# Ragged softmax on one core: a 32-column clip beside a GpSimd fill, and whole-tile stores

## The chip, the core and the metric

The kernel runs on one NeuronCore of a Trainium2 chip. The core has five engines with an instruction queue each: TensorE (PE), VectorE (DVE), ScalarE (ACT), GpSimd (POOL) and SyncE (SP), and 16 DMA engines that carry all transfers between the chip's memory (HBM) and the on-chip memory (SBUF, 128 partitions). The metric is the device time of one execution in microseconds. Before the change it is 154.53 us, the median of three runs that lie between 154.44 and 154.55 us.

## What is computed

```python
x: (16, 8, 256, 256) float32        # batch, heads, rows, columns
lengths: (16,) int32                # each from 128 to 255, the same draw each time
result = zeros_like(x)
for b in range(batch):
    length = lengths[b]
    masked = x[b, :, :, :length]
    exp_masked = exp(masked - max(masked, axis=-1))
    result[b, :, :, :length] = exp_masked / sum(exp_masked, axis=-1)
```

Each row of 256 numbers becomes a softmax over its first `length` columns and zero behind them. The kernel leaves the maximum out: it takes exp of x itself, checks the sums at the end, and has a slow second pass for the case that a sum is out of bounds. With this input the second pass is not entered.

## The kernel before, in words

**Tiles.** One batch entry is one tile: 2048 rows, 16 on each of the 128 partitions, 256 columns, 2 MB, contiguous 16 KB on each partition. Sixteen tiles are worked through in positions 0 to 15 (`batch_of` says which batch entry stands at a position). They lie in eight slots of SBUF, position b in slot b modulo 8. `half` is 8 of the 16 rows of a partition, `quarter` is 4. The constant `ahead` is 4, `low` is 160, `mid` is 128, `late` is 13.

**Loads.** Position 0 is loaded by SP in two halves (line 145), positions 1 to 3 whole by POOL (line 196). From position 4 on, POOL loads only the first w columns of each row (line 168), w being the first of 160, 168, ..., 240 that is not under the length, or all 256. POOL reads the length into a register (line 210, which calls line 135), chooses w by branches, and waits until the load two positions earlier has landed (line 167) and until the tile that had the slot is stored (line 209). So two loads at most are under way, in one queue, q0. Columns from 160 on of slots 4 to 7 are set to zero once by four memsets (line 191), so that what stands behind w is finite.

**Compute.** For each tile DVE applies a mask (line 248): it takes the minimum of x and a line that is far above zero inside the length and far below it outside, over columns 128 to 255 of all 16 rows, 2048 elements for each partition. ACT takes exp (lines 374 and 377), for rows 4 to 15 one row at a time with the row's sum; DVE sums the first four rows itself (line 269). DVE then divides, half a tile at a time: a reciprocal of the sums (line 279) and a multiplication (line 282). The loop at line 292 fixes the order on DVE, for every position b but 1: divide(b, 0), mask(b + 1), divide(b, 1), total(b + 1). DVE works in this order alone, so divide(b, 1) stands behind the mask of the next tile, and with it behind the landing of the next load.

**Stores.** SP issues all stores (line 154) in order of position, into queue q1. `parts(b)` cuts a tile: position 0 in pieces of 2, 2, 4 and 8 rows, positions 1 to 7 in pieces of 8, 4 and 4, positions 8 to 12 and 15 in two halves, positions 13 and 14 whole. A piece waits until the half in which it ends is divided (line 149). Positions 2 to 12 also wait until the store two positions earlier has landed (line 153), and position 0 has a wait of its own: from its second piece on, until the mask of position 1 is through (line 151). At the end SP waits for the last stores (lines 158, 159, 407).

Of the kernel before, what the change touches and what calls it, by code (L numbers as in the profile page):

```python
# [9 lines left out]
F32 = mybir.dt.float32  # L10
BF16 = mybir.dt.bfloat16
I32 = mybir.dt.int32
ALU = mybir.AluOpType
AX = mybir.AxisListType.X
EXP = mybir.ActivationFunctionType.Exp
DVE = mybir.EngineType.DVE
# [5 lines left out]
def kernel(  # L22
# [6 lines left out]
    nc = tc.nc  # L29
    P = nc.NUM_PARTITIONS  # L30

    batch, heads, seq_q, seq_k = x.shape
    rows = heads * seq_q
    assert rows % P == 0
    nt = rows // P
    half = nt // 2
    quarter = nt // 4
# [8 lines left out]
    slots = 8  # L46
    ahead = 4
    assert ahead == 4 and slots == 8 and batch == 16

    def batch_of(pos):  # L50
        return pos + 1 if pos < ahead - 1 else {ahead - 1: 15, 15: 0}.get(pos, pos)
# [3 lines left out]
    low = widths[0]  # L55
    mid = seq_k // 2
    big = 1.0e30

    def parts(b):


        if b == 0:
            cuts = [0, 2, quarter, half, nt]
        elif b < 8:
            cuts = [0, half, half + quarter, nt]
        elif b < 13 or b == batch - 1:
            cuts = [0, half, nt]
        else:
            cuts = [0, nt]
        return [slice(i, j) for i, j in zip(cuts, cuts[1:])]  # L70

    pool = ctx.enter_context(tc.tile_pool(name="all", bufs=1))
    psum = ctx.enter_context(tc.tile_pool(name="psum", bufs=1, space=bass.MemoryType.PSUM))
    xt = pool.tile([P, slots, nt, seq_k], F32, name="xt")
    word64 = pool.tile([1, batch], mybir.dt.int64, name="word64")
    word = word64.bitcast(I32)
# [3 lines left out]
    len_s = pool.tile([P, batch], F32, name="len_s")  # L80
    iota_i = pool.tile([P, seq_k], I32, name="iota_i")
    down = pool.tile([P, seq_k], F32, name="down")
    row_sum = pool.tile([P, slots, nt], F32, name="row_sum")
    inv_sum = pool.tile([P, batch, nt], F32, name="inv_sum")
    warm = pool.tile([P, 1], F32, name="warm")
# [20 lines left out]
    with tc.tile_critical(no_gpsimd_drain=True):  # L106
# [9 lines left out]
        s_fill = sem("s_fill")  # L116
        s_v = sem("s_v")
        s_min = sem("s_min")
# [14 lines left out]
        def length(engine, at):  # L133

            return nc.values_load(
                at,
                engines=[engine],
                skip_runtime_bounds_check_because="compared with constants, never an address",
            )
# [3 lines left out]
        for h in range(2):  # L143
            s = slice(h * half, (h + 1) * half)
            nc.sync.dma_start(out=xt[:, 0, s], in_=x_f[batch_of(0), :, s]).then_inc(s_ld[h], 16)  # L145
        for b in range(batch):
            s_b = s_st[b % 2] if b < late else s_late if b < batch - 1 else s_last
            for s in parts(b):
                nc.sync.wait_ge(s_out, 2 * b + (s.stop - 1) // half + 1)
                if b == 0 and s.start == 2:  # L150
                    nc.sync.wait_ge(s_min, 3)
                if 2 <= b < late and s.start == 0:
                    nc.sync.wait_ge(s_b, 64 * (b // 2 + 2))
                nc.sync.dma_start(
                    out=out_f[batch_of(b), :, s, :], in_=xt[:, b % slots, s, :]
                ).then_inc(s_b, 16 * (1 if b == 0 else (s.stop - s.start) // quarter))
        for par in range(2):
            nc.sync.wait_ge(s_st[par], n_st[par])
        nc.sync.wait_ge(s_late, 64 * (batch - 1 - late))
# [3 lines left out]
        def pick(v, b, slot, par, ws, landed):  # L163

            if len(ws) == 1:
                w = ws[0]
                nc.gpsimd.wait_ge(s_sw[par], landed)
                nc.gpsimd.dma_start(  # L168
                    out=xt[:, slot, :, :w], in_=x_n[:, b, :, :w]
                ).then_inc(s_sw[par], 16)  # L170
                return
            m = (len(ws) - 1) // 2
            with nc.gpsimd.If(v <= ws[m]):
                pick(v, b, slot, par, ws[: m + 1], landed)
            with nc.gpsimd.Else():
                pick(v, b, slot, par, ws[m + 1 :], landed)
# [8 lines left out]
        nc.gpsimd.memset(ones_c, 1.0).then_inc(s_ones, 1)  # L185
        for par in range(2):
            nc.gpsimd.memset(seed[:, par : par + 1], 0.0).then_inc(s_st[par], 128)  # L187
        nc.gpsimd.wait_ge(s_v, 2)

        def fill(b):  # L190
            nc.gpsimd.memset(xt[:, b, :, low:], 0.0).then_inc(s_fill, 1)  # L191


        fill(ahead)
        for b in range(1, ahead):
            nc.gpsimd.dma_start(out=xt[:, b], in_=x_f[batch_of(b)]).then_inc(  # L196
                s_sw[b - 1] if b < 3 else s_ld[2], 16
            )
        nc.gpsimd.wait_ge(s_word, 16)
        for b in range(ahead + 1, slots):  # L200
            fill(b)
        nc.gpsimd.wait_ge(s_fill, slots - ahead)


        with nc.Fori(16, 16 * (batch // 2 - 1), 16, engines=[POOL]) as landed:
            for par in range(2):
                n = landed // 8 + (ahead - 2 + par)
                b = n % 15 if par == 1 else n
                nc.gpsimd.wait_ge(s_st[par], 4 * landed)
                v_len = length(POOL, word[0:1, bass.ds(2 * b, 1)])  # L210
                pick(v_len, bass.ds(b, 1), bass.ds(n % slots, 1), par, widths + [seq_k], landed)
# [11 lines left out]
        def step(ins):  # L223
            nonlocal v
            v += 1
            ins.then_inc(s_v, 1)
# [5 lines left out]
                out=down, in0=iota_i, scalar1=0.5, scalar2=-big, op0=ALU.add, op1=ALU.mult  # L232
            )
        )
        nc.vector.wait_ge(s_word, 16)
        nc.vector.tensor_copy(out=len_b, in_=word[:, ::2]).then_inc(s_lenb, 1)  # L236
        nc.vector.wait_ge(s_lenf, 1)
        step(
            nc.vector.tensor_scalar(  # L239
                out=len_s, in0=len_f, scalar1=big, scalar2=None, op0=ALU.mult  # L240
# [1 line left out]
        )  # L242
        nc.vector.wait_ge(s_v, v)

        def clip(b, s, lo, hi):

            t = xt[:, b % slots, s, lo:hi]
            return nc.vector.scalar_tensor_tensor(  # L248
                out=t,
                in0=down[:, None, lo:hi].to_broadcast([P, s.stop - s.start, hi - lo]),  # L250
                scalar=len_s[:, batch_of(b) : batch_of(b) + 1],
                in1=t,
                op0=ALU.add,
                op1=ALU.min,
            )

        def mask(b, s):
            if b == 0:
                nc.vector.wait_ge(s_ld[s.start // half], 16)
            elif b == ahead - 1:  # L260
                nc.vector.wait_ge(s_ld[2], 16)
            else:
                par = (b - 1 if b < ahead else b) % 2
                nc.vector.wait_ge(s_sw[par], 16 * max(b // 2, 1))
            clip(b, s, mid, seq_k).then_inc(s_min, 1)

        def total(b):
            nc.vector.wait_ge(s_lump, b + 1)
# [7 lines left out]
        def divide(b, h):  # L276
# [10 lines left out]
            ).then_inc(s_out, 1)  # L287

        mask(0, slice(0, half))
        mask(0, slice(half, nt))  # L290
        total(0)
        for b in range(batch):


            first = b != 1
            if first:
                divide(b, 0)
            if b + 1 < batch:
                mask(b + 1, slice(0, nt))
            if not first:  # L300
                divide(b, 0)
            divide(b, 1)
            if b + 1 < batch:
                total(b + 1)
# [14 lines left out]
        for k, (_, _, edge, op) in enumerate(checks):  # L319
            nc.vector.tensor_scalar(  # L320
                out=bad[:, k : k + 1],
                in0=ends[:, k : k + 1],
                scalar1=edge,
                scalar2=None,
                op0=op,
# [9 lines left out]
        with nc.vector.Else():  # L335
            with nc.Fori(0, batch, 1, engines=[DVE]) as i:
                nc.vector.wait_ge(g_ld, 16 * i + 16)
                nc.vector.scalar_tensor_tensor(
                    out=g_t,
                    in0=down[:, None, :].to_broadcast([P, nt, seq_k]),  # L340
                    scalar=len_s[:, bass.ds(i, 1)],
                    in1=g_t,
                    op0=ALU.add,
                    op1=ALU.min,
# [3 lines left out]
                    out=neg_max, in_=g_t, op=ALU.max, axis=AX, negate=True  # L348
# [5 lines left out]
                    out=g_t,  # L354
                    in0=g_t,
# [9 lines left out]
        with nc.Fori(0, batch // slots, 1, engines=[ACT]) as turn:  # L365
            for slot in range(slots):
                for h in range(2):
# [7 lines left out]
                    for j in range(h * half + lump * (1 - h), (h + 1) * half):  # L375
                        e = xt[:, slot, j, :]
                        ins = nc.scalar.activation(  # L377
                            out=e, in_=e, func=EXP, accum_out=row_sum[:, slot, j : j + 1]
# [5 lines left out]
        with nc.scalar.If(a_redo >= 1):  # L384
# [4 lines left out]
            with nc.Fori(0, batch, 1, engines=[ACT]) as i:  # L389
                nc.scalar.dma_start(out=g_t, in_=x_g[:, bass.ds(i, 1)]).then_inc(g_ld, 16)  # L390
                nc.scalar.wait_ge(g_v, 3 * i + 2)
                with nc.Fori(0, nt, 1, engines=[ACT]) as t:
                    e = g_t[:, bass.ds(t, 1), :]
                    nc.scalar.activation(
                        out=e,
                        in_=e,
# [41 lines left out]
```

## Time and profile before

| what | value |
|---|---|
| median of three runs | 154.53 us (154.44 to 154.55) |
| the profiled execution: span, first to last instruction | 152.8 us |
| outside the span, by the median | 1.7 us |
| DVE busy | 134.6 us, 107 instructions |
| ACT busy | 95.1 us |
| POOL busy | 21.3 us |
| moved by DMA | 61.57 MB (read 27.98, written 33.55), 403 GB/s over the span |

The span is one execution under the profiler; what it lacks to the measured time lies before its first and after its last instruction. The page of the profile gives the busy time of each engine, then the span in 40 slices with a digit for each (9 is 90% busy or more), then the DMA queues with packets, megabytes and the share of the 16 engines' time that their packets took. The lines themselves are shown below, where they are used.

### The profile page before, as it was taken

The numbers are of one execution on the slowest core, as the hardware profiler recorded it, in microseconds if no ns is written. First come the engines' busy times: TensorE is split into PE (matmuls) and PEld (weight loads), VectorE is DVE, ScalarE is ACT, GpSimd is POOL, SyncE is SP. The second block draws the span as 40 slices with busy tenths as digits, with TensorE's granted clock in tenths as the row PEclk, the third lists the DMA queues.
The fourth block names the chain that finished last, engine by engine and source line by source line (L and its number), as shares of the span: only waits on it lengthen the run. The fifth ranks groups of instructions, "written<-read, shape, count | busy, mean of one in ns | idle before, by whom it ended". The sixth has DMA issues, their size and how long they took to land.

```text
span 152.8 us, 818 instructions
## 1 busy us (share of the span) xinstructions
PE 0.3 (0%) x2; PEld 0.2 (0%) x2; DVE 134.6 (88%) x107; ACT 95.1 (62%) x402; POOL 21.3 (14%) x29
## 2 busy tenths in 40 slices
PE   0000000000000000000000000000000000000000
PEld 0000000000000000000000000000000000000000
DVE  1369999999999999999999999999999999999500
ACT  3096699339394967859393939577593939395000
POOL 4962110030303020030300220302000000000000
DMA  4999999999999999999999999999999999999994
GB/s 107 420 446 433 401 435 347 421 445 420 394 397 422 405 421 411 411 409 405 419 411 418 408 399 419 408 410 423 417 421 419 413 420 422 435 435 442 429 410 187
DMA packets 10646, 61.57 MB, mean 403 GB/s; under 512 B 898, under 2 KB 1010, under 8 KB 7058
## 3 DMA queue, kind: packets, MB, share of 16 engines
q1 hardware_dynamic: 5904, 35.65, 56.7%
q0 software_dynamic: 4736, 25.89, 41.9%
q14 instruction: 4, 0.03, 0.1%
q10 hardware_dynamic: 2, 0.00, 0.0%
HBM read 27.98 MB, written 33.55 MB: 403 GB/s over the span
## 4 chain that ended last, share of the span: by engine, by line
DVE 87%; DMA 5%; issue 1%; SPq 0%; PE 0%
DVE xt L282 48%; DVE xt L248 23%; DVE row_sum L269 12%; DMA xt<-in_x_dram 5%; DVE inv_sum L279 3%; DVE ends L317 0%; SPq L145 0%; DVE bad L320 0%; PE count L218 0%; DVE redo L328 0%; SPq L433 0%; SPq L106 0%
## 5 line engine op out<-in xcount | busy, mean ns | idle before, releaser
L377 ACT ACTIVATE xt<-xt 128x256 f32<-128x256 f32 x192 | 76.6, 400 | 0.2 <-DVE xt L248 0.2
L282 DVE TENSOR_TENSOR xt<-xt,inv_sum 128x2048 f32<-128x2048 f32 x32 | 73.3, 2292 | 1.1
L374 ACT ACTIVATE xt<-xt 128x1024 f32<-128x1024 f32 x16 | 16.9, 1056 | 42.8 <-DVE xt L248 42.8
L248 DVE SCALAR_TENSOR_TENSOR xt<-down,len_s,xt 128x2048 f32<-128x2048 f32 (+1 forms) x17 | 37.7, 2219 | 5.0 <-DMA xt<-in_x_dram 5.0
L377 ACT ACTIVATION_READ_ACCUMULATOR xt<-xt 128x1 f32 x192 | 35.9, 187 | 0.0
L168 POOL DMA_DIRECT2D xt<-in_x_dram x12 | 13.2, 1104 | 84.0 <-DMA xt<-in_x_dram 62.3
L269 DVE TENSOR_REDUCE row_sum<-xt 128x4 f32<-128x1024 f32 x16 | 19.4, 1210 | 0.0
L279 DVE RECIPROCAL inv_sum<-row_sum 128x8 f32<-128x8 f32 x32 | 6.3, 198 | 0.5
L191 POOL MEMSET xt<- 128x1536 f32 x4 | 5.4, 1398 | 1.1 <-DVE len_s L239 1.1
L361 ACT ACT_TABLE_LOAD x1 | 1.3, 1283 | 1.6 <-SPq L106 1.6
L196 POOL DMA_DIRECT2D xt<-in_x_dram x3 | 1.8, 590 | 0.0
L231 DVE TENSOR_SCALAR down<-iota_i 128x256 f32<-128x256 int32 x1 | 0.3, 300 | 1.6 <-POOL iota_i L181 1.6
L317 DVE TENSOR_REDUCE ends<-inv_sum 128x1 f32<-128x256 f32 x2 | 0.7, 408 | 0.0
L236 DVE CAST len_b<-word 1x16 bf16<-1x16 int32 x1 | 0.2, 164 | 0.4 <-DMA word<-in_lengths_dram 0.4
L239 DVE TENSOR_SCALAR len_s<-len_f 128x16 f32<-128x16 f32 x1 | 0.2, 176 | 0.3 <-PE len_f L216 0.3
L218 PE MATMUL count<-bad,ones_c 128*1 128x3 bf16 x1 | 0.2, 165 | 140.8 <-DVE bad L320 140.8
L181 POOL IOTA iota_i<- 128x256 int32 x1 | 0.3, 331 | 0.6 <-SPq L106 0.6
L328 DVE TENSOR_REDUCE redo<-count 1x1 f32<-1x3 f32 x1 | 0.1, 150 | 0.3 <-PE count L218 0.3
L320 DVE TENSOR_SCALAR bad<-ends 128x1 bf16<-128x1 f32 x3 | 0.3, 150 | 0.0
L187 POOL MEMSET seed<- 1x1 f32 x2 | 0.2, 225 | 0.0
L218 PEld LDWEIGHTS count<-bad,ones_c 128*1 128x1 bf16 x1 | 0.1, 79 | 140.8 <-DVE bad L320 140.8
L361 ACT ACTIVATE warm<-const-float32-0.0 128x1 f32<-128x1 f32 x1 | 0.2, 204 | 0.0
(10 smaller groups left out, 1.1 us busy)
## 6 DMA issues: line engine op xcount, KB each, us to landing
out_dram<-xt SPq DMA_DIRECT2D x20, 1024.0 KB
xt<-in_x_dram POOLq DMA_DIRECT2D x4, 2048.0 KB, 16.3
out_dram<-xt SPq DMA_DIRECT2D x15, 512.0 KB
xt<-in_x_dram POOLq DMA_DIRECT2D x3, 1728.0 KB, 16.7
out_dram<-xt SPq DMA_DIRECT2D x2, 2048.0 KB
xt<-in_x_dram POOLq DMA_DIRECT2D x2, 1600.0 KB, 16.0
xt<-in_x_dram POOLq DMA_DIRECT2D x2, 1280.0 KB, 14.7
xt<-in_x_dram SPq DMA_DIRECT2D x2, 1024.0 KB, 6.4
```

What stands on the lines that cost most here:

```text
L168: nc.gpsimd.dma_start(out=xt[:, slot, :, :w], in_=x_n[:, b, :, :w]).then_inc(s_sw[par], 16)
L191: nc.gpsimd.memset(xt[:, b, :, low:], 0.0).then_inc(s_fill, 1)
L196: nc.gpsimd.dma_start(out=xt[:, b], in_=x_f[batch_of(b)]).then_inc(s_sw[b - 1] if b < 3 else s_ld[2], 16)
L218: nc.tensor.matmul(count, lhsT=ones_c, rhs=bad, start=True, stop=True).then_inc(s_count, 1)
L248: return nc.vector.scalar_tensor_tensor(out=t, in0=down[:, None, lo:hi].to_broadcast([P, s.stop - s.start, hi - lo]), scalar=len_s[:, batc ...
L269: nc.vector.tensor_reduce(out=row_sum[:, b % slots, :lump], in_=xt[:, b % slots, :lump, :], op=ALU.add, axis=AX,).then_inc(s_exp[0], 1)
L279: step(nc.vector.reciprocal(out=inv_sum[:, b, s], in_=row_sum[:, b % slots, s]))
L282: nc.vector.tensor_tensor(out=t, in0=t, in1=inv_sum[:, b, s, None].to_broadcast([P, half, seq_k]), op=ALU.mult,).then_inc(s_out, 1)
L317: step(nc.vector.tensor_reduce(out=ends[:, k : k + 1], in_=values, op=op, axis=AX))
L361: nc.scalar.activation(out=warm, in_=nc.const_aps.tensor(0.0, (P, 1), F32), func=EXP)
L374: nc.scalar.activation(out=e, in_=e, func=EXP).then_inc(s_lump, 1)
L377: ins = nc.scalar.activation(out=e, in_=e, func=EXP, accum_out=row_sum[:, slot, j : j + 1])
```

## The change

The change has three parts.

- **The narrow mask.** For positions from 4 on DVE clips only 32 columns (`edge` = 160 - 128), which begin at the tile's length, or at 224 if that is less. DVE reads the first column into a register from a small tile `first_col`, which one new instruction computes at the start. What stands behind w is filled by GpSimd: right behind each narrow load POOL copies a constant of -1e30 over columns w to 255 of the 16 rows (for a full load, a dummy copy of one column). The mask waits for that fill on the semaphore `s_fill`. Of the four memsets at the start, one stays for slot 4, now with -1e30, and a small one makes the constant.
- **Whole stores.** `parts` cuts only positions 0 and 15, in two halves; all others are stored whole, with 16 KB on each partition.
- **No hold.** The wait of position 0's second piece for the mask of position 1 goes.

```diff
     def parts(b):
-        if b == 0:
-            cuts = [0, 2, quarter, half, nt]
-        elif b < 8:
-            cuts = [0, half, half + quarter, nt]
-        elif b < 13 or b == batch - 1:
+        if b in (0, batch - 1):
             cuts = [0, half, nt]
         else:
             cuts = [0, nt]
...
                 nc.sync.wait_ge(s_out, 2 * b + (s.stop - 1) // half + 1)
-                if b == 0 and s.start == 2:
-                    nc.sync.wait_ge(s_min, 3)
                 if 2 <= b < late and s.start == 0:
                     nc.sync.wait_ge(s_b, 64 * (b // 2 + 2))
...
                 nc.gpsimd.dma_start(
                     out=xt[:, slot, :, :w], in_=x_n[:, b, :, :w]
                 ).then_inc(s_sw[par], 16)
+                m = max(seq_k - w, 1)
+                nc.gpsimd.tensor_copy(
+                    out=xt[:, slot, :, w:] if w < seq_k else spent[:, : nt, None],
+                    in_=never[:, None, :m].to_broadcast([P, nt, m]),
+                ).then_inc(s_fill, 1)
                 return
...
-        nc.gpsimd.wait_ge(s_v, 2)
-        def fill(b):
-            nc.gpsimd.memset(xt[:, b, :, low:], 0.0).then_inc(s_fill, 1)
-        fill(ahead)
+        nc.gpsimd.wait_ge(s_v, 3)
+        nc.gpsimd.memset(xt[:, ahead, :, low:], -big).then_inc(s_fill, 1)
+        nc.gpsimd.memset(never, -big).then_inc(s_fill, 1)
...
-        for b in range(ahead + 1, slots):
-            fill(b)
-        nc.gpsimd.wait_ge(s_fill, slots - ahead)
+        nc.gpsimd.wait_ge(s_fill, 2)
...
+        step(
+            nc.vector.tensor_scalar(
+                out=first_col, in0=word[:, ::2],
+                scalar1=seq_k - edge, scalar2=0, op0=ALU.min, op1=ALU.max,
+            )
+        )
...
         def mask(b, s):
+            cols, n = slice(mid, seq_k), seq_k - mid
+            if b >= ahead:
+                k = batch_of(b)
+                cols, n = bass.ds(length(DVE, first_col[0:1, k : k + 1]), edge), edge
+                nc.vector.wait_ge(s_fill, b - ahead + 3)
...
-            clip(b, s, mid, seq_k).then_inc(s_min, 1)
+            clip(b, s, cols, n).then_inc(s_min, 1)
```

More of the change, by code (lines that the diff above doesn't have):

```diff
@@ L57 @@
     big = 1.0e30
+    edge = low - mid
     def parts(b):
-        if b == 0:
-            cuts = [0, 2, quarter, half, nt]
-        elif b < 8:
-            cuts = [0, half, half + quarter, nt]
-        elif b < 13 or b == batch - 1:
+        if b in (0, batch - 1):
             cuts = [0, half, nt]
@@ L82 @@
     down = pool.tile([P, seq_k], F32, name="down")
+    never = pool.tile([P, seq_k - low], F32, name="never")
+    spent = pool.tile([P, nt], F32, name="spent")
+    first_col = pool.tile([1, batch], I32, name="first_col")
     row_sum = pool.tile([P, slots, nt], F32, name="row_sum")
@@ L155 @@
                     out=out_f[batch_of(b), :, s, :], in_=xt[:, b % slots, s, :]
-                ).then_inc(s_b, 16 * (1 if b == 0 else (s.stop - s.start) // quarter))
+                ).then_inc(s_b, 16 * (s.stop - s.start) // quarter)
         for par in range(2):
@@ L236 @@
         nc.vector.tensor_copy(out=len_b, in_=word[:, ::2]).then_inc(s_lenb, 1)
+        step(
+            nc.vector.tensor_scalar(
+                out=first_col,
+                in0=word[:, ::2],
+                scalar1=seq_k - edge,
+                scalar2=0,
+                op0=ALU.min,
+                op1=ALU.max,
+            )
+        )
         nc.vector.wait_ge(s_lenf, 1)
@@ L243, with clip @@
         nc.vector.wait_ge(s_v, v)
-        def clip(b, s, lo, hi):
-            t = xt[:, b % slots, s, lo:hi]
+        def clip(b, s, cols, n):
+            t = xt[:, b % slots, s, cols]
             return nc.vector.scalar_tensor_tensor(
                 out=t,
-                in0=down[:, None, lo:hi].to_broadcast([P, s.stop - s.start, hi - lo]),
+                in0=down[:, cols][:, None, :].to_broadcast([P, s.stop - s.start, n]),
                 scalar=len_s[:, batch_of(b) : batch_of(b) + 1],
```

## The prediction, made before the changed kernel was run

> **What bounds the kernel now.** I read the page first: its head, its slices, its queues and its chain.
>
> ```profile
> span 152.8 us, 818 instructions
> ...
> DMA  4999999999999999999999999999999999999994
> ...
> q1 hardware_dynamic: 5904, 35.65, 56.7%
> q0 software_dynamic: 4736, 25.89, 41.9%
> ...
> DVE 87%; DMA 5%; issue 1%; SPq 0%; PE 0%
> ```
>
> The chain names DVE. But the DMA row is full in every slice but the ends, and the two queues take 98.6% of the 16 engines' span. So I cut the span into stages (columns: engine busy times, clock, DMA share, GB/s) and looked at the first and last packet.
>
> ```profile
> 15.00:127.00 112.00, 0.00 (x0) 0.00 (x0) 110.66 (x81) 77.45 (x329) 12.76 (x12) 1.00 1.02 412
> 127.00:144.00 17.00, 0.17 (x1) 0.08 (x1) 16.39 (x19) 10.21 (x47) 0.00 (x0) 1.00 1.02 432
> ...
> 1.14 0.86 SPq L145 DMA_DIRECT2D xt<-in_x_dram  x2
> ...
> q1 hardware_dynamic: 7, 0.06, 254.2%
> ...
> DMA packets 0, 0.00 MB, mean 0 GB/s; under 512 B 0, under 2 KB 0, under 8 KB 0
> ```
>
> The last two rows are the queue in 2.15 to 2.30 us (its first seven packets, 1.0 us after SP's issue at 1.14) and the queues in 151.3 to 152.8 (nothing). From 2.15 to 151.3 the engines carry packets without a gap, at a share of 1.02 (packets overlap a little). So the end is set by **DMA: 149.1 us of transfers**, with 2.15 us in front and 1.5 us behind. DVE is also nearly always busy, but its last store is only queued behind others: the stores waited for earlier stores 11 times, 86.6 us in all.
>
> ```profile
> SPq L153 <- DMA out_dram<-xt: 86.6, 11, 9.9
> ...
> DVE xt L248 <- DMA xt<-in_x_dram: 5.0, 2, 3.5
> ```
>
> The second row says that masks waited for loads only twice, at the start. So before, DVE never starves, and behind it stands a backlog of stores, which keeps DMA full to the end.
>
> **Part one, the narrow mask.** Rows of the groups by form (mean ns), then one tile on DVE in the chain.
>
> ```profile
> L248 DVE SCALAR_TENSOR_TENSOR xt<-down,len_s,xt 128x2048 f32<-128x2048 f32 x15 | 35.2, 2344 | 0.0
> L248 DVE SCALAR_TENSOR_TENSOR xt<-down,len_s,xt 128x1024 f32<-128x1024 f32 x2 | 2.6, 1284 | 5.0 <-DMA xt<-in_x_dram 5.0
> ...
> 131.61 2.26 DVE xt L248
> 133.87 0.12 DVE inv_sum L279
> ...
> 134.02 2.29 DVE xt L282
> 136.31 1.14 DVE row_sum L269
> ...
> 137.47 0.21 DVE inv_sum L279
> ...
> 137.71 2.29 DVE xt L282
> 140.00 0.12 DVE inv_sum L279
> ```
>
> The two sizes give 1.035 ns an element and 0.22 us fixed, so 512 elements take 0.75 us; 1.59 us goes, 12 times, 19.1 us of DVE. A tile costs DVE 8.39 us now (131.61 to 140.00) and 6.8 after. A tile costs DMA 2.10 MB of store and of load, without q0's four full ones, (25.89 - 4 x 2.10) / 11 = 1.6 MB: 3.7 MB at 412 GB/s is 9.0 us. DVE is therefore not what ends last, and by itself this gain is **worth nothing**. It does have an effect: DVE eats its backlog. How far loads lead the masks shows in two tiles:
>
> ```profile
> 19.49 0.54 POOL L168 DMA_DIRECT2D xt<-in_x_dram  x1 [3.81 <-DMA xt<-in_x_dram]
> ...
> xt<-in_x_dram POOLq DMA_DIRECT2D x1, 2048.0 KB, 20.1
> 47.61 2.34 DVE L248 SCALAR_TENSOR_TENSOR xt<-down,len_s,xt 128x2048 f32<-128x2048 f32 x1
> ...
> 106.21 1.15 POOL L168 DMA_DIRECT2D xt<-in_x_dram  x1 [6.97 <-issue]
> ...
> xt<-in_x_dram POOLq DMA_DIRECT2D x1, 1536.0 KB, 21.0
> ```
>
> Position 5 lands at 19.49 + 20.1 = 39.6 and is masked at 47.6: a lead of 8.0 us. Position 15 lands at 127.2 and is masked at 131.6: 4.4. Saving 1.59 a tile uses up 8 us after five tiles. From about position 9 each mask waits for its load.
>
> The new register load on DVE: the only one in this trace took 0.84 us (row below). It stands ahead of the waits, so it runs on DVE's sequencer beside the 2.29 us of the division in front, or during the wait for the load. Uncovered it costs 12 x 0.84 = 10.1 us of DVE, still less than 19.1, and 0.8 on the path at the very end. I take 0. The new wait for the fill holds divide(b, 1) behind it. The fill is issued right behind its load, which takes 13.4 us at least to land. Three memsets of 1536 elements took 4.04 us, 1.35 each; a copy of 16 to 1536 elements I put between 0.1 and 2.7 (twice that), covered either way. POOL has the room: it stands idle 84.0 us before its loads. The three memsets that go and the small instruction for `first_col` have SP's first loads beside them (q1 holds the engines alone until 7.6, a row below): 0.
>
> ```profile
> L135 DVEq TENSOR_LOAD <-redo x1: 842/842/842, 143.9 to 143.9; - x1
> ...
> DMA to landing us min/median/max: 13.4/16.8/21.0
> ...
> 6.12 4.04 POOL L191 MEMSET xt<- 128x1536 f32 x3
> ...
> L168 POOL DMA_DIRECT2D xt<-in_x_dram x12 | 13.2, 1104 | 84.0 <-DMA xt<-in_x_dram 62.3 <-issue 15.5 <-DMA out_dram<-xt 6.1
> ```
>
> **Part two, whole stores.** First the packets' price. Queue rows of three stretches: 49.5 to 55 (stores in 4 KB packets beside loads), 146.6 to 148.6 (8 KB, stores alone), 142 to 145.5 (16 KB, alone).
>
> ```profile
> q0 software_dynamic: 292, 1.18, 53.2%
> q1 hardware_dynamic: 289, 1.08, 48.6%
> ...
> q1 hardware_dynamic: 114, 0.85, 100.9%
> ...
> q1 hardware_dynamic: 94, 1.47, 97.8%
> ```
>
> Bytes over size give 264, 104 and 90 data packets; share x stretch x 16 over these gives 0.162, 0.310 and 0.609 us. A partition's 16 KB cost 0.310 + 2 x 0.162 = 0.634 us in positions 1 to 7, 0.620 in 8 to 12, and 0.609 whole. Each engine has 8 partitions: 7 x 8 x 0.025 + 5 x 8 x 0.011 = 1.84 us. Position 0 loses its two 2 KB packets (0.09 each by the same line): 8 x (2 x 0.09 + 0.162 - 0.310) = 0.2. In all **2.0 us less transfer**; bounds 1.5 and 2.5 from rounding of the rows.
>
> The Trainium skill, "SBUF — State Buffer", section "The DMA setup-cost knee", puts about 2 us on each transfer and asks for the largest single ones; 23 stores fewer would then bring an estimated 46 us by that page. The stretch 146.6 to 148.6 speaks against it: two stores meet there and the share stays at 100.9%, so a queued store pays nothing of the kind.
>
> Then who gets DMA. In 49.5 to 55 the two queues move 292 and 289 packets. In 47.5 to 49.5, with 8 KB stores, they move these:
>
> ```profile
> q1 hardware_dynamic: 65, 0.53, 63.6%
> q0 software_dynamic: 71, 0.31, 38.0%
> ```
>
> **The queues alternate packet by packet, whatever their size.** Against a narrow load's 4.4 KB (0.31 MB / 71) a 16 KB store packet takes 79% of the bytes, an 8 KB one 63%. While a whole store runs, a load crawls at about 90 GB/s. Nothing is lost by that while both queues hold work, but loads are late and stores early: the opposite of a backlog of stores.
>
> **What is late next.** With loads late, DVE stands at mask(b + 1), and behind it divide(b, 1), and behind that the whole store of b. (Before, the first half could go alone.) At the last load this costs DMA time: when position 15 lands, positions 14 and 15 are not stored, all else is or nearly is. Work until then is all but two stores (2 x 8 x 0.609 = 9.8): 2.15 + 149.1 - 2.0 - 9.8 = 139.5, and the landing is seen a little later (at the end of the run between 0 and 1.5 us, the stretch from the last packet to the end of the span); I take 0.3, so 139.8. Then mask 0.75, divide(14, 1) 2.44 by the chain above, 1.0 from issue to first packet: store 14 starts at 144.05. DMA idles **4.5 us**. Store 14 runs to 148.95. Divide(15, 0) ends at 143.0 + 1.14 + 2.55 = 146.7 and divide(15, 1) at 149.15; their halves start at 148.95 and 151.4 without a gap and end at 153.85. With 1.5 behind, the span is 155.35.
>
> **Part three, no hold** lets 1 MB of store run beside loads 2 and 3, 2.5 us at most (8 x 0.310); it makes DVE wait under 1 us early, where it has 19 us to spare: 0.
>
> **The sum:** -2.0 + 4.5 = +2.5 us on the profile's 152.8, and the same on the median, whose 1.7 us outside the span do not change: **157.0 us**.
>
> **Rivals.**
> *Backlog stays (faster).* If at the last landing 4.5 us of store packets are still queued, nothing idles and only the 2.0 us count: 152.5. That is so if loads keep their share, for instance if a 16 KB packet is cut at 4 KB before queues alternate. Against it speak the equal counts at 8 KB, and the stretch 17 to 23 us, where 16 KB loads ran beside small pieces of store:
>
> ```profile
> q0 software_dynamic: 155, 2.28, 93.2%
> q1 hardware_dynamic: 114, 0.23, 9.9%
> ```
>
> The bytes stood 10 to 1; with cuts at 4 KB, 2 KB pieces would have had a third. What speaks for it: no 16 KB store runs beside a narrow load in this trace, so the share there is extrapolated. The Trainium skill, "DMA: Bandwidth & Descriptors", section "SWDGE vs HWDGE vs iDMA", has a packet at 4096 B preferably, as "the DMA engine's context-switching boundary"; by that sentence the time would be this rival's, and the two rows do not bear it out. Chance 0.17.
> *Part of the gap (same).* Load 15 has only some 22 packets an engine (1.57 MB / 4.4 KB / 16). If it lands right behind load 14, store 13 is itself held (it starts 0.75 + 2.44 + 1.0 = 4.2 behind mask 14) and covers part. Mask 15 then follows divide(14, 0), 0.75 + 2.44 + 1.14 + 2.55 = 6.9 behind mask 14; store 14 starts at 6.9 + 4.2 = 11.1, store 13 ended at 4.2 + 4.9 = 9.1: 2.0 us idle there. With 2.0 saved: 154.5. Chance 0.11.
> *More gaps (slower still).* POOL asks for load n + 2 only when load n has landed, and q0's first packet came over 3.2 us behind its issue at 4.37 (below; 7.0 to 7.6 holds q1 alone). A narrow load alone takes about 3.9 us (1.6 MB at 412). If the request takes 4 to 5 us, each time that no store runs beside, q0 falls dry for up to 1 us, some four times: 159 to 161. Chance 0.10.
>
> ```profile
> 4.37 1.76 POOL L196 DMA_DIRECT2D xt<-in_x_dram  x3
> ...
> q1 hardware_dynamic: 31, 0.25, 99.8%
> ```
>
> **Chances and range.** My forecast with 1.5 to 2.5 saved and 3.5 to 5.5 idle, 155.5 to 158.5, has 0.62. Slower by over 0.2% (0.3 us, about what a measurement can tell) 0.72, within 0.11, faster 0.17. The range that leaves out no more than 2 in 10 takes in the part gap and stops ahead of the pure gain: 153.8 to 159.4.
>
> **What would show it.** Right: mask 0.75 us; masks from about position 9 on wait for loads; the last load lands at 135 or later instead of 127; a slice near 140 with DMA far under 9; equal packet counts with stores at 80% of the bytes. Wrong: DMA full to the end, or DVE's masks never waiting.

## The result, and the profile after

The changed kernel takes **159.02 us** (median of five runs, 158.89 to 163.42) against 154.53 us before: a ratio of 1.0286, with a 95% interval of 1.0272 to 1.0301. It is slower by 4.5 us where +2.5 us was forecast. The changed kernel has a second, slower state, 161 us and more, in some of its runs; the ratios leave it out, and the rows below are of the same kernel in a run of 159.38 us with a span of 157.8 us. These are the page's head, DMA slices and queues.

```profile
span 157.8 us, 915 instructions
...
DMA  4999999999999999999999999999999999995994
...
q1 hardware_dynamic: 2880, 35.65, 54.0%
q0 software_dynamic: 4736, 25.89, 43.1%
```

The same megabytes went through the same queues. Share times span gives the time that one engine spent on each queue: the stores' q1 took 86.6 us before (56.7% of 152.8) and 85.2 now, **1.4 less**; the loads' q0 took 64.0 and now 68.0, **4.0 more**. And one slice near the end is down to 5. The waits on DVE and the last piece of DMA in the chain:

```profile
DVE xt L255 <- DMA xt<-in_x_dram: 16.3, 9, 4.3
```

```profile
122.56 17.89 DMA xt<-in_x_dram
140.45 0.03 issue
140.48 0.02 DVEq L276
...
141.52 0.75 DVE xt L255
...
142.42 2.29 DVE xt L294
```

By this row masks wait for loads nine times, where before it was twice. The last load lands at 140.45 in place of 127.2. The narrow mask takes 0.75 us, but starts 1.07 us after the landing: DVE's sequencer works out the address of the 32 columns (rows of line 255 with a q) behind the wait. The stretch from 143 to 146 us, in the changed kernel and before (second last column the DMA share):

```profile
143.00:146.00 3.00, 0.00 (x0) 0.00 (x0) 2.96 (x3) 3.00 (x15) 0.00 (x0) 1.00 0.43 183
```

```profile
143.00:146.00 3.00, 0.17 (x1) 0.08 (x1) 0.60 (x6) 0.00 (x0) 0.00 (x0) 1.00 0.99 423
```

That is an idle stretch of 3.0 x (1 - 0.43) = 1.7 us, while DVE divides the second half of tile 14 (the row at 142.42) and ACT works on tile 15. So of the 5.0 us between the two spans, 2.6 are dearer transfers (4.0 - 1.4) and 1.7 the gap; about 0.7 is left over, in the overlap of packets and in smaller idle stretches behind the last landing.

### The profile page after: what moved, and what is told of

The parts are those of the page before. It is cut to its first block, busy times and chain, and to the rows that moved or that the text cites. A ratio compares the mean times of both kernels' runs of the same rounds, so it can differ in the third digit from the quotient of the medians.

```text
span 159.7 us, 915 instructions
## 1 busy us (share of the span) xinstructions
PE 0.3 (0%) x2; PEld 0.2 (0%) x2; DVE 126.4 (79%) x108; ACT 95.0 (59%) x402; POOL 33.5 (21%) x39
## 4 chain that ended last, share of the span: by engine, by line
DMA 84%; DVE 7%; issue 3%; POOL 1%; POOLq 1%; DVEq 0%; PE 0%; ACTq 0%; SPq 0%
DMA xt<-in_x_dram 83%; DVE xt L294 4%; POOL xt L193 1%; DMA word<-in_lengths_dram 1%; DVE row_sum L281 1%; POOLq L166 1%; DVE xt L255 0%; DVE ends L329 0%; DVE inv_sum L291 0%; DVEq L255 0%; POOLq L135 0%; DVE bad L332 0%; DVE len_s L246 0%; PE count L215 0%; PE len_f L213 0%
## 5 line engine op out<-in xcount | busy, mean ns | idle before, releaser
L294 DVE TENSOR_TENSOR xt<-xt,inv_sum 128x2048 f32<-128x2048 f32 x32 | 79.9, 2498 | 1.1
L255 DVE SCALAR_TENSOR_TENSOR xt<-down,len_s,xt (+2 forms) x17 | 22.2, 1305 | 23.5 <-DMA xt<-in_x_dram 19.0
L170 POOL COPY xt<-never 128x640 f32 (+6 forms) x11 | 15.1, 1373 | 0.0
L193 POOL MEMSET xt<- 128x1536 f32 x1 | 1.4, 1388 | 1.1 <-DVE len_s L246 1.1
L170 POOL COPY spent<-never 128x16 f32<-128x16 f32 x1 | 1.1, 1092 | 0.0
```

What stands on the lines that cost most here:

```text
L170: nc.gpsimd.tensor_copy(out=xt[:, slot, :, w:] if w < seq_k else spent[:, : nt, None], in_=never[:, None, :m].to_broadcast([P, nt, m]),).t ...
L193: nc.gpsimd.memset(xt[:, ahead, :, low:], -big).then_inc(s_fill, 1)
L255: return nc.vector.scalar_tensor_tensor(out=t, in0=down[:, cols][:, None, :].to_broadcast([P, s.stop - s.start, n]), scalar=len_s[:, batch ...
L294: nc.vector.tensor_tensor(out=t, in0=t, in1=inv_sum[:, b, s, None].to_broadcast([P, half, seq_k]), op=ALU.mult,).then_inc(s_out, 1)
```

## The experiments

Two theories went into the first four runs. **Theory A** is the prediction's: large store packets delay the loads, and DMA idles at the last load. **Theory B**: the cost lies in the new steps of the narrow mask. Ratios are to runs of the kernel before on the same chip, with the 95% interval.

**The changed kernel again**, unchanged.

> The changed kernel once more, for a profile of an ordinary run. Theory A (stores in 16 KB packets take four fifths of the DMA time while they run, loads come late, the mask of the next tile holds the division and the whole store, and DMA idles at the last load): 158.9 to 159.2 us, last load landed at 138 or later, masks waiting for loads, one idle stretch of DMA near the end of some 2 to 5 us. Theory B (the cost lies in the new steps of the narrow mask on DVE and GpSimd): the same time, and the sum of the waits of DVE that are not for a landing explains some 4 us.

It took 158.74 and 159.38 us. The gap is 1.7 us, a little under what A names. As B would have it, the profile has 4.5 us of waits of masks that it does not put down to a landing:

```profile
DVE xt L255 <- issue: 4.5, 2, 3.0
```

But both stand behind landings. The shorter is the last mask's, shown above. The longer ends with the mask of position 6 at 59.63 us, 0.35 us behind POOL's issue of the load that waits for the landing of the same tile. So after the start masks wait for their loads at positions 6 to 9 and 13 to 15, and these waits do not speak for B. The next runs test it by itself.

**The narrow mask alone.** The lines of `parts`, the hold and the semaphore increments are as before, all else as changed.

```diff
-        if b in (0, batch - 1):
-            cuts = [0, half, nt]
+        if b == 0:
+            cuts = [0, 2, quarter, half, nt]
+        elif b < 8:
+            cuts = [0, half, half + quarter, nt]
+        elif b < 13 or b == batch - 1:
+            cuts = [0, half, nt]
```

> The narrow mask with the fill alone; stores and the hold as before. Theory A: loads keep their share beside 8 and 4 KB store packets, a backlog of stores is left at the last load, so within 0.5 us of before: 154.0 to 155.0 us. Theory B: the new steps cost here too, 157 to 159 us.

155.75 us, ratio 1.008 (1.0054 to 1.0106): B is out. The narrow mask costs 0.8%, somewhat over A's upper end. The last load, from its row in the chain, landed at 106.29 + 20.92 = 127.2, as before, and by the page the engines' time on the queues did not change (64.1 and 86.7 us).

```profile
106.29 20.92 DMA xt<-in_x_dram
```

```profile
span 153.4 us, 937 instructions
...
q1 hardware_dynamic: 5904, 35.65, 56.5%
q0 software_dynamic: 4736, 25.89, 41.8%
```

**Whole stores alone**, the wide mask kept.

```diff
-        if b == 0:
-            cuts = [0, 2, quarter, half, nt]
-        elif b < 8:
-            cuts = [0, half, half + quarter, nt]
-        elif b < 13 or b == batch - 1:
+        if b in (0, batch - 1):
             cuts = [0, half, nt]
...
-                if b == 0 and s.start == 2:
-                    nc.sync.wait_ge(s_min, 3)
```

> Whole stores without the hold; the wide mask as before. Theory A: loads are late by the larger packets already here, DVE (8.4 us a tile) leaves less room, so slower than before: 156 to 158 us. Theory B: only the 2.0 us of packets count, 152.5 us.

159.27 us, ratio 1.0298 (1.028 to 1.0316): **the whole loss, without the narrow mask.** It is over A's range. Loads took 67.9 us of engine time here too, without GpSimd's copies.

```profile
span 157.9 us, 796 instructions
...
q1 hardware_dynamic: 2880, 35.65, 53.9%
q0 software_dynamic: 4736, 25.89, 43.0%
```

```profile
143.00:146.70 3.70, 0.00 (x0) 0.00 (x0) 3.63 (x5) 3.65 (x14) 0.00 (x0) 1.00 0.30 128
```

The gap is 3.7 x 0.70 = 2.6 us.

**Halves.** The changed kernel with every tile in two stores of 8 KB packets (`cuts = [0, half, nt]` for all).

> The changed kernel with every tile stored in two halves, in 8 KB packets. Theory A: loads get 35% of the bytes beside a store in place of 20%, and the first half of a tile is not held by the next mask: 155 to 156.5 us. Theory B: as the changed kernel and some 0.7 us more for packets, 159.5 us.

159.36 us, ratio 1.0277 (1.0223 to 1.033): a miss for A. Transfers are nearly at the old price (65.0 and 86.5 us by the page's queues), but the last load, in the chain, landed at 123.23 + 19.06 = 142.3, and the gap is longer than in the changed kernel: 4.0 x (1 - 0.24) = 3.0 us in one stretch. The last slices of its DMA row are only 5, 6 and 8 tenths busy, so more is idle around it.

```profile
span 158.1 us, 929 instructions
...
q1 hardware_dynamic: 4896, 35.65, 54.7%
q0 software_dynamic: 4736, 25.89, 41.1%
```

```profile
123.23 19.06 DMA xt<-in_x_dram
```

```profile
144.00:148.00 4.00, 0.00 (x0) 0.00 (x0) 3.90 (x6) 3.86 (x16) 0.00 (x0) 1.00 0.24 100
```

So there were two costs, and A had only one of them. **Theory C**: a packet of a narrow load is dearer when no store packet runs beside it, and large stores leave most load packets alone; in addition, late loads open the gap. **Rival D**: something else makes the loads dear. **Rival E**: the missing hold makes them late.

**Loads alone.** No compute; SP waits for all loads and then stores sixteen tiles. It leaves out the softmax.

```diff
-        for b in range(batch):
-            s_b = s_st[b % 2] if b < late else s_late if b < batch - 1 else s_last
-            for s in parts(b):
...
+        for par in range(2):
+            nc.sync.wait_ge(s_sw[par], 16 * (batch // 2 - 1))
+        for b in range(batch):
+            nc.sync.dma_start(out=out_f[batch_of(b)], in_=xt[:, b % slots]).then_inc(s_last, 16)
```

> Only the transfers of the kernel before: the loads as they are (two narrow ones under way at most), no compute and no store until all have landed, then sixteen whole stores; it leaves out the softmax. Theory C (a narrow load packet is dearer when no store packet runs beside it): packets of 4,320 bytes at 185 to 195 ns where before has 171, the narrow loads at 350 to 375 GB/s, 16 KB packets at 611 to 625 ns as ever. Rival D (the dearer packets of the changed kernel come from something else, the fill or the late phase of the run): 171 ns and 400 GB/s.

By the page, q0 took 42.6% of 169.2 us, **72.1 us in place of 64.0 for the same packets**. The rows of DMA's queues for a stretch of narrow loads alone, here from 59 to 65 us, beside the changed kernel's from 92 to 97, where no store ran either:

```profile
q0 software_dynamic: 523, 2.18, 101.4%
```

```profile
q0 software_dynamic: 435, 1.82, 102.0%
```

Share x stretch x 16 over the packets gives 0.186 and 0.188 us, 358 and 357 GB/s for a queue that has the engines to itself. In the kernel before, 292 packets at 53.2% of 5.5 us took 0.160 each, 403 GB/s (1.18 MB over the share's time). The full loads of the first positions, in packets of 16 KB, were not slow alone: from 10 to 22 us of the loads alone, 5.18 MB over 100.7% of 12 us is 429 GB/s.

```profile
q0 software_dynamic: 348, 5.18, 100.7%
```

The sizes of the packets are not the reason: in the traces' records the 1,200 load packets of 4,320 bytes took 0.171 us each in the mean before, 0.182 in the changed kernel and 0.196 here. C holds, and only for the narrow packets; GpSimd's copies are not the cause.

**Quarters.** The changed kernel with all stores in 4 KB packets (`cuts = [0, quarter, half, half + quarter, nt]`).

> The changed kernel with every tile stored in four pieces of 4 KB packets. Theory A and C: loads get half of the bytes beside a store, load packets are back at 171 to 197 ns, no mask waits after the start, last load landed near 120 us, no gap of DMA; what is left is the price of 4 KB packets, 0.648 in place of 0.634 and 0.620 us for 16 KB, some 2.8 us in all: 156.8 to 157.8 us. Rival E (the narrow mask's steps or the missing hold make the loads late): load landings as in the changed kernel, 159 us or more.

157.59 us, ratio 1.0207 (1.0179 to 1.0235), the last load, in the chain, at 108.75 + 13.53 = 122.3, no gap. A and C have the time right, E is out; but the masks of positions 14 and 15 still wait, 2.8 us in all, where none was to. Load time is back at 64.3 us; stores cost 89.4, 2.8 more than before, which is most of the loss.

```profile
108.75 13.53 DMA xt<-in_x_dram
```

```profile
span 156.0 us, 961 instructions
...
DMA  4999999999999999999999999999999999999992
...
q1 hardware_dynamic: 9504, 35.66, 57.3%
q0 software_dynamic: 4736, 25.89, 41.2%
```

**The hold put back**, with position 0's old cuts, in the changed kernel.

> The changed kernel with position 0 cut and held as before. Theory A and C: the hold lies 120 us ahead of the gap and is made up for long before, 158.5 to 159.5 us. Rival E: 155 to 156.5 us.

158.64 us, ratio 1.0261 (1.0218 to 1.0305): no difference that can be told from 1.0286.

**Small pieces first, whole later.** The narrow mask and the hold; positions 1 to 8 in pieces of 8, 4 and 4, from 9 on whole.

> The narrow mask and the hold, positions 1 to 8 in pieces of 8, 4 and 4 rows, 9 to 14 whole. Theory C: the loads are far enough ahead by then that a backlog of stores covers the end and each narrow load still runs beside a store for most of its time, 154.0 to 155.0 us; if the lead is used up after all, 156 to 158 us.

155.41 us, ratio 1.0054 (1.0037 to 1.0071): 0.4 above the range. Queue times by the page are those of before (64.0 and 86.6 us), and it lies level with the narrow mask alone. It is the nearest that any version came to the kernel before.

```profile
span 153.9 us, 934 instructions
...
q1 hardware_dynamic: 5472, 35.65, 56.3%
q0 software_dynamic: 4736, 25.89, 41.6%
```

**Whole first, small pieces later**: positions 1 to 7 whole, 8 to 14 in pieces.

> The changed kernel with the order of sizes turned round: positions 1 to 7 whole, 8 to 14 in pieces of 8, 4 and 4 rows. Theory C (two prices: narrow load packets are dear while they run alone, and DMA idles at the last load): the loads run alone in the first half and cost some 1 to 2 us more, the small packets then let them catch up, no gap at the end: 155.0 to 156.5 us. If the gap alone made the changed kernel slow: 154.0 to 154.5 us. If whatever comes early decides: 158 us or more.

157.69 us, ratio 1.0224 (1.0182 to 1.0265): above C's range. There is no gap (16 us at the end at a share of 1.02) and still a loss of 3.2 us of span: 66.9 us for loads, 86.1 for stores. C named 1 to 2 us for the loads alone; it is 2.9. The price of lonely loads is thus a cost by itself.

```profile
137.00:153.00 16.00, 0.17 (x1) 0.08 (x1) 10.98 (x16) 6.23 (x27) 0.00 (x0) 1.00 1.02 424
```

**Both halves divided before the next mask**, in the changed kernel from position 3 on.

```diff
             if first:
                 divide(b, 0)
+            if b >= ahead - 1:
+                divide(b, 1)
             if b + 1 < batch:
                 mask(b + 1, slice(0, nt))
             if not first:
                 divide(b, 0)
-            divide(b, 1)
+            if b < ahead - 1:
+                divide(b, 1)
```

> The changed kernel with both halves divided before the next tile's mask, from position 3 on, so that no store waits for a load. Step of the prediction (the division held behind the mask makes the gap): the store of position 14 is out before the last load lands and the gap gets shorter, 156.5 to 158 us. Theory C (the last tile's own chain is what DMA waits for, and loads stay dear): DVE now waits for ACT in each tile, the gap is as long or longer, 158 to 161 us.

163.75 us, ratio 1.0605 (1.0588 to 1.0623), above both ranges. Two gaps, 4.0 x 0.98 = 3.9 and 5.0 x 0.38 = 1.9 us, stand in the tail:

```profile
144.50:148.50 4.00, 0.00 (x0) 0.00 (x0) 3.16 (x3) 0.74 (x5) 0.00 (x0) 1.00 0.02 6
153.00:158.00 5.00, 0.16 (x1) 0.08 (x1) 4.05 (x9) 1.18 (x6) 0.00 (x0) 1.00 0.62 254
```

The old order is the better one: in the new one DVE waits for ACT in every tile, 24.7 us in all.

```profile
DVE row_sum L281 <- ACT xt L389: 13.5, 12, 1.1
DVE inv_sum L291 <- ACT xt L392: 11.2, 23, 0.7
```

The last load landed at 122.95 + 17.9 = 140.9 us, but the last mask began at 147.56: DVE and ACT set the pace of the tail here, at 9.1 us a tile, and not the load. So this run does not test the held division. The changed kernel's own rows bear on it:

```profile
137.80 2.29 DVE L294 TENSOR_TENSOR xt<-xt,inv_sum 128x2048 f32<-128x2048 f32 x1
```

This is divide(14, 0). It ends at 140.09, and ACT was through with tile 14 at 139.84, so divide(14, 1) could have begun then. It began at 142.42, 2.3 us later, behind the landing, the address and the mask, and the gap is 1.7 us. That agrees with the prediction's step; no run takes this hold away by itself.

**Two load queues.** Transfers alone again, odd positions loaded by SP. It leaves out the softmax.

> Transfers alone again, narrow loads in two queues: even positions from GpSimd, odd ones from SP, two of each under way, widths written out; it leaves out the softmax. If an engine with only one queue to serve is what makes a narrow packet dear: 4,320-byte packets at 171 to 180 ns as beside stores. If it needs a store beside it (reads from the chip's memory beside writes to it): 196 ns or more, as in the run of loads alone.

SP's queue cut narrow loads into packets of under 1 KB, so the mix is not the one meant. DMA's queues from 43 to 57 us:

```profile
q0 software_dynamic: 1025, 4.33, 84.4%
q1 hardware_dynamic: 1023, 0.86, 19.5%
```

q0's 0.184 us a packet, 366 GB/s, with another queue's packet behind nearly each: hardly cheaper than alone. That speaks for the second reading of the expectation, that it takes writes beside the reads; SP's small packets leave it short of shown.

**First columns written out**, so that DVE computes no address.

```diff
-                cols, n = bass.ds(length(DVE, first_col[0:1, k : k + 1]), edge), edge
+                cols, n = slice(starts[k], starts[k] + edge), edge
```

> The changed kernel with the first columns of the narrow masks written out, so that DVE loads and computes no register for them. If the 1.06 us that DVE's sequencer spent between the last landing and the last mask is on the path: the idle stretch of DMA near the end shrinks from 1.7 to about 0.7 us, 157.7 to 158.2 us. If it is hidden, as the prediction had it, or if loads only shift by it: 158.7 to 159.3 us. Either way the load packets stay dear and the kernel stays slower than before by over 3 us.

In the profiled run, one of 162.49 us, the step is gone from the chain (the landing at 124.81 + 19.71 = 144.52, the mask at 144.61). But the kernel's six runs scatter from 158.61 to 163.91 us, ratio 1.0347 (1.0296 to 1.0399), over both ranges. What the 1.07 us are worth stays open.

```profile
124.81 19.71 DMA xt<-in_x_dram
...
144.61 0.75 DVE xt L256
```

## Why the prediction was right in sign, and which step failed

**DMA is the bound, DVE's 19 us are worth nothing**: right, by the narrow mask alone (+0.8%, not faster). Where its loss comes from, 0.6 us in the two spans, is not settled; queue times are the same. The 19 us themselves were too many: DVE's busy time fell from 134.6 to 127.3 us. Part of what the masks save goes to the divisions, which GpSimd's copies slow (last section). These are their groups before and in the changed kernel:

```profile
L282 DVE TENSOR_TENSOR xt<-xt,inv_sum 128x2048 f32<-128x2048 f32 x32 | 73.3, 2292 | 1.1
L294 DVE TENSOR_TENSOR xt<-xt,inv_sum 128x2048 f32<-128x2048 f32 x32 | 79.2, 2476 | 1.1
```

**"In all 2.0 us less transfer"** is the step that failed. The stores gave 1.4. The term that the prediction put at nothing is the loads': +4.0, so that transfers are dearer by 2.6. The prediction had every load packet priced beside a store, since the trace of before has no other: it alternates one for one all the way. The queues from 20 us to the last load's end, before (to 126) and changed (to 140):

```profile
q1 hardware_dynamic: 4393, 22.88, 52.7%
q0 software_dynamic: 4372, 20.72, 48.8%
```

```profile
q1 hardware_dynamic: 2006, 27.44, 54.2%
q0 software_dynamic: 4429, 21.37, 47.0%
```

Before, there is a store packet for each load packet. With 16 KB packets there are 2,006 for 4,429, so 2,423 load packets at least must run alone, whatever the order. At 0.187 us in place of 0.160 that makes an estimated 2,423 / 16 x 0.027 = 4.1 us for each engine, against the 4.0 measured. The prediction had counted packets for shares, and could have seen this; their price alone no row of before shows.

**Packet by packet, whatever the size**: right. From 86 to 90 us of the changed kernel:

```profile
q1 hardware_dynamic: 81, 1.33, 77.7%
q0 software_dynamic: 80, 0.32, 20.1%
```

Equal counts, 81% of the bytes to the store (79% forecast). The rival by which 16 KB are cut at 4 KB is out; the sentence of the Trainium skill, "DMA: Bandwidth & Descriptors", section "SWDGE vs HWDGE vs iDMA", on a packet of preferably at most 4096 B as the switching boundary stands in its table on what GpSimd builds, and does not describe these stores, which SP issues.

**Late loads**: right (140.4, forecast 139.8). Masks wait, though not from position 9 to the end but at 6 to 9 and 13 to 15. The reason was only half right. With the narrow mask alone just the masks of positions 14 and 15 wait, 4.2 us in all; with whole stores and the wide mask those of 6, 7, 10 and 14 do. So whole stores make the loads late, and no run shows that DVE's saving eats the backlog of stores.

**The 4.5 us gap**: right in kind, mis-sized. It measured 1.7, since store 13 still ran when the last load landed (q1 alone moved 1.29 MB from 140 to 143 us), as the rival "part of the gap" described. The stretches quoted above give 2.6 us with whole stores alone and 3.0 with halves. That the held division makes it agrees with the rows of the changed kernel, but is not shown by a run: the other order cost 4.7 us more, by waits of its own.

**The register load at 0**: the load itself lay ahead of the wait, but the address arithmetic, 1.07 us, did not. **No hold at 0**: right, by the hold put back. In the aside on the fixed cost of a transfer the count is off: SP issues 39 stores before and 18 after, 21 fewer and not 23. The start of store 14 adds up to 143.99, not 144.05; neither changes the forecast.

So +2.5 was -2.0 + 4.5, and the measured 5.0 of span were +2.6 + 1.7 + 0.7. The direction was right for one of its reasons, the gap; without the loads' price, which the prediction did not have, a gap of 1.7 and 2.0 saved would have come out level. That 159.02 still lies in the range, 0.4 us under its upper end, owes something to luck: it is outside the forecast's own 155.5 to 158.5. It falls in the span of the rival "more gaps", but not by its mechanism, since no slice of the DMA row between the first and the tail is under 9.

## What to carry to other kernels

Where DMA is full, price a change in packets of each queue, not in bytes: two busy queues alternate one for one, so making one queue's packets larger slows the other and leaves it alone for longer. Look whether the trace shows the price of a packet that runs alone before pricing it as if in company. And an engine that is not the bound brings nothing by getting faster: the narrow mask alone ran at 1.008.

## What the runs showed of the hardware

A narrow load's packet (rows of 640 to 896 bytes, gathered to some 4.4 KB) runs at 403 GB/s beside stores and at 357 alone; packets of 16 KB, without short rows, ran at 429 alone. Why a lone narrow packet is dearer stays open.

GpSimd's copy slows DVE. A mask of 512 elements took 0.75 us, and a division 2.29, with no copy beside them; beside a copy (timeline of the changed kernel, start, duration, engine):

```profile
97.95 1.48 POOL L170 COPY xt<-never 128x1536 f32 x1
```

```profile
97.64 2.35 DVE L255 SCALAR_TENSOR_TENSOR xt<-down,len_s,xt  x1
...
103.83 3.03 DVE L294 TENSOR_TENSOR xt<-xt,inv_sum 128x2048 f32<-128x2048 f32 x1
```

The second fell beside the next tile's copy, from 104.80 to 107.64 us. The Trainium skill, "GPSIMD Engine Reference", section "Specifications", says that GpSimd shares its SBUF interfaces with VectorE and contends with DVE instructions that have two SBUF inputs; both of these have, and the rows agree, 1.6 us and 0.7 us more. Beside GpSimd's memsets nothing was seen. Those of the kernel before, which read nothing, ran beside a mask of 1024 elements, from 6.12 to 10.16 us, that took no longer than the group's mean of 1.28:

```profile
6.46 1.28 DVE L248 SCALAR_TENSOR_TENSOR xt<-down,len_s,xt 128x1024 f32<-128x1024 f32 x1 [3.47 <-DMA xt<-in_x_dram]
```
